# Row factors through DRAM in place of diagonal products and a second turn of k, in a hybrid encoder layer on one core

## The chip, the core and the metric

The kernel runs on one core of a Trainium2 chip. The metric is the device time of one launch in microseconds; a smaller number is better. The engines are named PE (TensorE), DVE (VectorE), ACT (ScalarE), POOL (GpSimd) and SP (SyncE, which here issues DMAs alone). Each engine takes its instructions in the order in which the program has them, and waits where one of them waits.

## The reference

One layer, 512 tokens of 2048 channels, all in float32.

```python
h = rms_norm(x, norm_g[layer])
proj = jnp.einsum('bsd,de->bse', h, w_in[layer])
qa, ka, va, ga, qb, kb, vb, gb = jnp.split(proj, splits, axis=-1)
ya = stick_breaking_attention(...)      # branch A, 8 heads of 128
yb = chunk_band_attention(...)          # branch B, 8 heads of 128
mixed = jnp.concatenate([merge_heads(ya) * jax.nn.silu(ga),
                         merge_heads(yb) * jax.nn.silu(gb)], axis=-1)
x = x + jnp.einsum('bse,ed->bsd', mixed, w_out[layer])
```

Two factors of this matter here. `rms_norm(x)` divides each token by the root of its mean square: one number a token, here called `rstd`. In branch B, `chunk_band_attention` begins with `q = rms_norm(q, q_gain)` and `k = rms_norm(k, k_gain)`, over the 128 channels of a head: again one number a token, for each head.

## The kernel before, in words

The two large products, with `w_in` and with `w_out`, make up nearly all of PE's work. Each number is split into a high and a low part, and a product is made of three of the four products of parts; blocks are combined by a Winograd scheme with seven products in place of eight. The product with `w_in` is cut into 32 units (8 groups of two heads; in each group q, k, v and gate), and most units are 7 stages of 16 matmuls (L866 and L868 in the profile). For each stage, weights are loaded from DRAM by SP (L520, L536), some are summed by a DMA that POOL issues (L540, L559) or by DVE (L548), then ACT makes the high part (L579) and DVE the low part (L580), which is called a split here. DVE and ACT also bring the products out of the banks of PSUM and combine them (L612 to L649).

Odd groups belong to branch B, even ones to branch A. The attention of a head runs beside the large product of later units, on three spare banks. A head's number is n = 2g + h for group g and h = 0 or 1.

The projections come out with channels on the 128 partitions and 512 tokens along the row (`C`). A factor by token is then a number by column, and no engine's operand by partition can hold it. The kernel before deals with that in two ways:

- `R` is `rstd` as a row, the same in all partitions: [128, 512]. `x_rstd` makes four diagonal blocks out of `rstd` (L1277), PE multiplies a block of ones with them (L1284, in `spread`), and DVE copies the bank into `R`. All that takes R into account waits for it.
- For q and k of branch B, `prep_b` turns the head on PE, so that tokens lie on the partitions (four transposes of 128 x 128, L1429, reading `c`); ACT squares the turned head and sums along the row (L1434), and small operations of 4 columns make the factor `y` (L1442, L1443, `rsqrt` with L1226 to L1233, L1447). For k, ACT then scales the turned head by `y` into a buffer `tm` (L1461), and PE turns it back (L1429 again, reading `tm`). `heads` splits the result into high and low part (L1470, L1471).

For q the factor goes into the softmax and needs no row.

The order of all engines is made when the program is built. A planner (`schedule`) plays the work through with a cost for each operation and a clock of its own; on each engine it takes the ready operation that is due first. An `Op` on SP counts as done when its bytes and a landing time have gone by. `landing(us)` holds a piece of work back for some more time of that clock. What comes out is a fixed order on each engine; on the chip the instructions wait by semaphores. Weight loads are asked for about 10 us before their stage. `buffer(tag)` hands out room in the tags L (one buffer), W (three) and bias (one); `take` and `give` hand out the three spare banks.

`done.add(("read", n, kind))` marks that q (0) or k (1) of a head has been read out of `C`, whose tile the next group may then overwrite, and the next head's `prep_b` waits for it.

Of the kernel before, what the change touches and what calls it, by code (L numbers as in the profile page):

```python
# [8 lines left out]
F32 = mybir.dt.float32  # L9
# [68 lines left out]
def trunk_kernel(ctx: ExitStack, tc: tile.TileContext, xT, xn, wi, wqk, wo, ng, qg, kg, rel, out):  # L78
# [51 lines left out]
    halves = banks.rearrange("p a (b c) -> p (a b) c", c=H)  # L130
    mixd = [dp.tile([P, S], F32, tag=f"mixd{i}", name=f"mixd{i}") for i in range(2 * NG)]
# [1114 lines left out]
    def x_stat(t, i, k):  # L1246
        x = []

        def fn():
            x.append(tmp([P, S], "W", "xs", bufs=3))  # L1250
# [6 lines left out]
        drop("W", k)  # L1257
        done.add(("stat", t, i))

    def x_rstd():  # L1260
# [11 lines left out]
        ks = yield from buffer("W", 2)  # L1272
        o = tmp([P, P], "W", "ones", bufs=3)
        d = tmp([P, S], "W", "diag", bufs=3)
        yield G(0.3, lambda: pool.memset(o, 1.0))
        for t in range(NT):
            yield DV(128, lambda: dve.tensor_scalar(out=d[:, t * P:(t + 1) * P], in0=ident, scalar1=rstd[:, t:t + 1], scalar2=None,  # L1277
                                                   op0=ALU.mult), 0.0)
        i = yield from take("R")

        def spread():
            for t in range(NT):
                s_ = slice(t * P, (t + 1) * P)
                pe.matmul(banks[:, i, s_], o, d[:, s_], start=True, stop=True)  # L1284

        yield M(1.0, spread)
        for k in ks:
            drop("W", k)
        yield DV(512, lambda: dve.tensor_copy(R, banks[:, i, :]), 0.0)
        give(i)  # L1290
        done.add("R")
# [123 lines left out]
    def prep_b(g, kind, h):  # L1415
# [316 lines left out]
```

## Time and profile before

| | us |
|---|---|
| median of 3 runs | 901.56 (901.37 to 901.56) |
| profiled execution | 901.53 |
| its span, first to last instruction | 899.6 |

| engine | busy us | share of the span |
|---|---|---|
| PE | 892.7 | 99% |
| DVE | 767.7 | 85% |
| ACT | 658.8 | 73% |
| POOL | 69.9 | 8% |

The granted clock of PE is 1.00 throughout. The sixteen DMA engines move 177 GB/s on average. In a row of the profile, `L866 PE MATMUL banks<-x,parts ... xN | busy, mean | idle <-who` gives the source line, engine, operation, what is written and read, the count, the busy time in us and the mean duration of one in ns, then the idle time of the engine just before these and what ended it. A row of the timeline begins with the start in us and the length in us. Matmuls overlap: the next starts before the one ahead has ended. Of DMAs, the last number is the median time from issue to landing, in us.

### The profile page before, as it was taken

Reading aid. Unit: us, or ns where it says so; the run is one execution under the profiler, and the core shown is the slowest. Engines: PE = TensorE matmul, PEld = TensorE weight load, DVE = VectorE, ACT = ScalarE, POOL = GpSimd, SP = SyncE. Lnnn points to the kernel's source line nnn. Section 1 sums busy time; section 2 is a strip of 40 time slices with the busy share of each in tenths; the row PEclk is TensorE's granted clock in tenths of the full one; section 3 lists DMA queues with packets and bytes.
Section 4 is the critical chain, followed back from the end, with each engine's and each line's share of the span. In section 5 each row is a group of like instructions: output and inputs, shape, how many; then the busy total and the mean of one; then the engine's idle time right before and its main releaser. Section 6 shows DMA issues by size and latency. Waiting matters only on the chain.

```text
span 899.6 us, 15403 instructions
## 1 busy us (share of the span) xinstructions
PE 892.7 (99%) x5456; PEld 796.5 (89%) x5456; DVE 767.7 (85%) x1257; ACT 658.8 (73%) x1225; POOL 69.9 (8%) x96
## 2 busy tenths in 40 slices
PE   9999999999999999999999999999999999999998
PEld 7898888888888888888888888888888988999997
DVE  7998989787887977988889778888888988988785
ACT  7876968797698858986978588869878885544342
POOL 0001000000000000000000100000000000101012
PEclk9999999999999999999999999999999999999999
DMA  9777786868679888776878777868775536656371
GB/s 312 250 212 164 159 178 178 194 148 202 161 171 173 196 190 162 192 186 161 184 168 201 191 172 182 191 158 185 167 165 136 178 118 208 158 195 180 126 188 47
DMA packets 200509, 159.36 MB, mean 177 GB/s; under 512 B 21744, under 2 KB 170224, under 8 KB 200432
## 3 DMA queue, kind: packets, MB, share of 16 engines
q1 hardware_dynamic: 190352, 125.73, 48.1%
q0 software_dynamic: 9792, 32.51, 22.4%
q8 instruction: 43, 0.70, 0.3%
q14 instruction: 34, 0.28, 0.1%
q10 hardware_dynamic: 288, 0.14, 0.1%
HBM read 117.45 MB, written 8.39 MB: 140 GB/s over the span
## 4 chain that ended last, share of the span: by engine, by line
PE 95%; ACT 2%; DMA 1%; issue 1%; DVE 1%; SPq 0%; DVEq 0%; ACTq 0%
PE banks L866 39%; PE banks L795 21%; PE banks L868 19%; PE banks L793 10%; PE banks L1523 2%; PE banks L856 2%; PE banks L1429 1%; PE banks L857 1%; DMA arena<-in_wi 1%; ACT parts L579 0%; ACT W L1499 0%; DMA xq<-in_xT 0%; ACT W L1506 0%; PE banks L1355 0%; PE banks L1570 0%
## 5 line engine op out<-in xcount | busy, mean ns | idle before, releaser
L866 PE MATMUL banks<-x,parts 128*128 128x512 f32 x1568 | 501.1, 401 | 0.2 <-DVE arena L622 0.2
L868 PEld LDWEIGHTS banks<-x,parts 128*128 128x128 f32 x1568 | 294.3, 188 | 70.5 <-DVE parts L580 1.0
L868 PE MATMUL banks<-x,parts 128*128 128x256 f32 x1568 | 309.8, 279 | 0.3 <-DVE parts L580 0.3
L580 DVE TENSOR_TENSOR parts<-arena,parts 128x1024 fp32r<-128x1024 f32 x196 | 238.8, 1220 | 52.7 <-ACT parts L579 51.8
L579 ACT CAST parts<-arena 128x1024 fp32r<-128x1024 f32 x196 | 205.7, 1050 | 86.3 <-PE banks L866 46.2
L866 PEld LDWEIGHTS banks<-x,parts 128*128 128x128 f32 x1568 | 240.4, 189 | 1.3 <-issue 0.4
L795 PE MATMUL banks<-parts,x 128*128 128x256 f32 (+1 forms) x672 | 134.5, 298 | 0.0
L458 ACT CAST parts<-arena 128x1024 fp32r<-128x1024 f32 (+2 forms) x86 | 77.1, 908 | 69.2 <-PE banks L795 38.2
L795 PEld LDWEIGHTS banks<-parts,x 128*128 128x128 f32 x672 | 107.5, 191 | 3.7
L462 DVE TENSOR_TENSOR parts<-arena,parts 128x1024 fp32r<-128x1024 f32 (+2 forms) x86 | 89.0, 1044 | 14.5 <-ACT parts L458 14.5
L793 PE MATMUL banks<-parts,x 128*128 128x256 f32 (+1 forms) x336 | 100.3, 299 | 0.0
L548 DVE TENSOR_TENSOR arena<-arena 128x1024 f32<-128x1024 f32 x56 | 68.2, 1218 | 16.0 <-DMA arena<-in_wi 15.5
L795 PE MATMUL banks<-x,parts 128*128 128x256 f32 (+1 forms) x320 | 74.9, 326 | 0.1
L793 PEld LDWEIGHTS banks<-parts,x 128*128 128x128 f32 x336 | 63.9, 190 | 3.2
L795 PEld LDWEIGHTS banks<-x,parts 128*128 128x128 f32 x320 | 54.0, 190 | 5.6 <-DVE parts L462 0.7
L793 PE MATMUL banks<-x,parts 128*128 128x256 f32 (+1 forms) x160 | 52.9, 330 | 0.0
L540 POOL DMA_DIRECT2D arena<-arena x28 | 24.4, 873 | 327.9 <-DVE arena L622 71.8
L622 DVE TENSOR_TENSOR arena<-banks,arena 128x512 f32<-128x512 f32 x56 | 38.1, 681 | 5.3 <-PE banks L868 5.1
L559 POOL DMA_DIRECT2D arena<-arena x28 | 24.3, 868 | 232.2 <-DVE parts L580 178.3
L1532 DVE TENSOR_TENSOR wtl<-banks,wth 128x128 fp32r<-128x128 f32 (+1 forms) x64 | 31.0, 484 | 3.0 <-ACT wth L1531 2.8
L793 PEld LDWEIGHTS banks<-x,parts 128*128 128x128 f32 x160 | 30.5, 190 | 3.1 <-ACT parts L458 0.3
L1523 PE MATMUL banks<-ident,W 128*128 128x128 f32 x160 | 28.1, 274 | 0.8 <-ACT W L1508 0.7
(216 smaller groups left out, 1181.0 us busy)
## 6 DMA issues: line engine op xcount, KB each, us to landing
arena<-in_wi SPq DMA_DIRECT2D x308, 256.0 KB, 4.6
arena<-arena POOLq DMA_DIRECT2D x56, 512.0 KB, 5.7
arena<-in_wo SPq DMA_DIRECT2D x64, 256.0 KB, 3.1
xs<-in_xn SPq DMA_DIRECT2D x16, 256.0 KB, 4.2
mixd<-c SPq DMA_DIRECT2D x16, 256.0 KB, 3.5
out<-co SPq DMA_DIRECT2D x16, 256.0 KB, 4.6
x<-mixd SPq DMA_DIRECT2D x12, 256.0 KB, 4.0
co<-in_xn POOLq DMA_DIRECT2D x12, 256.0 KB, 6.0
```

The source lines that it names most:

```text
L458: act.copy(whl[n, part][:, 0, c], t)
L462: yield DV(c.stop - c.start, lambda: dve.tensor_tensor(out=l[:, c], in0=t, in1=h[:, c].bitcast(F32), op=ALU.subtract), need(k, 0.5))
L548: add = lambda x, due: DV(1024, lambda: dve.tensor_tensor(out=r("A21"), in0=r("A21"), in1=r(x), op=ALU.add), due)
L579: yield AC(1024, lambda: act.copy(v[:, 0, :], t), need(k, AHEAD[3]))
L580: yield DV(1024, lambda: dve.tensor_tensor(out=v[:, 1, :], in0=t, in1=v[:, 0, :].bitcast(F32), op=ALU.subtract), need(k, AHEAD[4]))
L622: join = lambda i, x, y, op=ALU.subtract: lambda: dve.tensor_tensor(out=c[:, i, :], in0=x, in1=y, op=op)
L793: pe.matmul(o, lh, rh, start=start, stop=False, **kw)
L795: pe.matmul(o, x, y, start=False, stop=stop and (x is ll) != early, **kw)
L866: pe.matmul(both, mats[n][:, 0, j, :], X[j][:, :, i, :], start=p in (0, 1, 5) and j == 0, stop=False, skip_group_check=True)
L868: pe.matmul(o[:, :H], mats[n][:, 1, j, :], X[j][:, 0, i, :], start=False, stop=j == NJ - 1, skip_group_check=True)
L1523: pe.transpose(t[:, j * P:(j + 1) * P], src[:, j * P:(j + 1) * P], ident)
L1532: yield DV(w, lambda: dve.tensor_tensor(out=tl[:, blocks, :], in0=tv, in1=th[:, blocks, :].bitcast(F32), op=ALU.subtract))
```

## The change

`as_row` is new. It writes the factor, a tile of 128 partitions and 4 columns, to a row of 512 numbers in DRAM (`rowd`, one for each head and one for `rstd`), waits, and reads that row back into all 128 partitions with a step of 0 between partitions. Both transfers are issued by SP.

- `R` comes from `as_row`; ones, diagonal blocks, their product and the copy are gone.
- k of branch B in groups 1, 3 and 5 is turned once, for its squares. The squares are written back into the bank, which is given back at once. The factor becomes a row (`kr`), DVE multiplies the unturned head in `C` by it in place, and `heads` reads `C` instead of the bank. Group 7 (`NG - 1`) keeps the two turns.
- q's squares go into the bank too, and need no buffer L.
- What the next `prep_b` waits for is a new mark, `squares`; `read` for k comes after `heads`.
- The 16 loads of x for `rstd` use buffers of the tags L and bias beside W: five in flight in place of three.

```diff
     def x_stats():
         yield lambda: position[0] > 18
         for t in range(NT):
             for i in range(4):
-                k, = yield from buffer("W")
-                spawn(x_stat(t, i, k), (0, 1))
+                tag = ("W", "W", "L", "W", "bias")[(4 * t + i) % 5]
+                k, = yield from buffer(tag)
+                spawn(x_stat(t, i, tag, k), (0, 1))
...
     def x_rstd():
...
-        ks = yield from buffer("W", 2)
-        o = tmp([P, P], "W", "ones", bufs=3)
-        d = tmp([P, S], "W", "diag", bufs=3)
-        yield G(0.3, lambda: pool.memset(o, 1.0))
-        for t in range(NT):
-            yield DV(128, lambda: dve.tensor_scalar(out=d[:, t * P:(t + 1) * P], in0=ident, scalar1=rstd[:, t:t + 1], scalar2=None,
-                                                   op0=ALU.mult), 0.0)
-        i = yield from take("R")
-
-        def spread():
-            for t in range(NT):
-                s_ = slice(t * P, (t + 1) * P)
-                pe.matmul(banks[:, i, s_], o, d[:, s_], start=True, stop=True)
-
-        yield M(1.0, spread)
...
-        yield DV(512, lambda: dve.tensor_copy(R, banks[:, i, :]), 0.0)
-        give(i)
+        yield from as_row(rstd, R, rowd[2 * NG])
         done.add("R")
+
+    def as_row(columns, row, at):
+
+        w = NT * P * 4
+        yield L_(w, lambda: sp.dma_start(at.rearrange("(t p) -> p t", p=P), columns, allow_slow_non_contiguous=True))
+        yield landing(0.3)
+        yield L_(P * 2048, lambda: sp.dma_start(row, bass.AP(tensor=at.tensor, offset=at.offset, ap=[[0, P], [1, S]])))
...
     def prep_b(g, kind, h):
...
-        yield lambda: all(("read", n - 1, k) in done for k in range(2)) if h else kind == 0 or ("read", n, 0) in done
-        yield lambda: not h or kind == 0 or ("read", n, 0) in done
-        k, = yield from buffer("L")
-        t_ = tmp([P, S], "L", "tm")
+        yield lambda: all(("squares", n - 1, k) in done for k in range(2)) if h else kind == 0 or ("squares", n, 0) in done
+        yield lambda: not h or kind == 0 or ("squares", n, 0) in done
         i = yield from take(("forth", g, kind, h))
...
+        by_rows = kind == 0 or g < NG - 1
+        o = b
+        if not by_rows:
+            k, = yield from buffer("L")
+            o = r = tmp([P, S], "L", "kr")
         for t in range(NT):
-            yield Op("ACT", 0.5, lambda: act.activation(t_[:, t * P:(t + 1) * P], b[:, t * P:(t + 1) * P], AF.Square,
+            yield Op("ACT", 0.5, lambda: act.activation(o[:, t * P:(t + 1) * P], b[:, t * P:(t + 1) * P], AF.Square,
                                                         accum_out=ssq[:, kind, h, t:t + 1]))
+        if by_rows:
+            give(i)
...
-        for t in range(NT):
-            yield Op("ACT", 0.37, lambda: act.activation(t_[:, t * P:(t + 1) * P], b[:, t * P:(t + 1) * P], AF.Copy, scale=y[:, t:t + 1]))
-        d = yield from qk_of(g, h)
-        yield M(0.5, lambda: turn_(t_))
-        drop("L", k)
-        yield from heads(n, 1, d, b, kg_t)
-        give(i)
...
+        k, = yield from buffer("L")
+        r = tmp([P, S], "L", "kr")
+        yield from as_row(y, r, rowd[n])
+        yield DV(512, lambda: dve.tensor_tensor(out=f, in0=f, in1=r, op=ALU.mult))
+        drop("L", k)
+        d = yield from qk_of(g, h)
+        yield from heads(n, 1, d, f, kg_t)
+        done.add(("read", n, 1))
```

Since the planner plays the whole program through again, the order changes on every engine, while the large products keep theirs. Three places are shown. In the changed file the lines of the stages are one higher (L866 becomes L867, L580 becomes L581), and the numbers behind `x_` differ by name alone.

On PE, the place in group 3 where the second turn of k of its first head stood. Before:

```order
L868 MATMUL banks<-x_143,parts 128x256
L868 MATMUL banks<-x_145,parts 128x256
L1429 MATMUL banks<-ident,tm 128x128 x4
L866 MATMUL banks<-x_204,parts 128x512
L866 MATMUL banks<-x_206,parts 128x512
```

Now, at the same place of the large product:

```order
L869 MATMUL banks<-x_160,parts 128x256
L869 MATMUL banks<-x_162,parts 128x256
L867 MATMUL banks<-x_221,parts 128x512
L867 MATMUL banks<-x_223,parts 128x512
L869 MATMUL banks<-x_221,parts 128x256
```

The four transposes are gone and nothing has come in their place.

On SP, where group 3's two heads have their rows made (`rowd` is the row in DRAM, `rq` the factor, `kr` the row in all partitions; the other rows are loads of weights, a store of a finished head and a DMA transpose of v). Now:

```order
L537 DMA arena<-in_wi 128x4x128 x2
L521 DMA arena<-in_wi 128x4x128 x6
L1280 DMA rowd_88<-rq 128x4x1
L521 DMA arena<-in_wi 128x4x128 x2
L1282 DMA kr<-rowd_88 128x512
L537 DMA arena<-in_wi 128x4x128 x2
L1544 DMA_TRANSPOSE vt<-c_3384 128x8x128
L521 DMA arena<-in_wi 128x4x128 x4
L1280 DMA rowd_89<-rq 128x4x1
L521 DMA arena<-in_wi 128x4x128 x2
L1282 DMA kr<-rowd_89 128x512
L521 DMA arena<-in_wi 128x4x128 x2
```

Before, the same stretch of loads was

```order
L536 DMA arena<-in_wi 128x4x128 x2
L520 DMA arena<-in_wi 128x4x128 x8
L536 DMA arena<-in_wi 128x4x128 x2
L1539 DMA_TRANSPOSE vt<-c_3362 128x8x128
L520 DMA arena<-in_wi 128x4x128 x8
```

Each write and its read stand among the weight loads, with two loads between them here, and everything behind the read is issued after it.

On DVE, the first head of group 3 again, from the last product of k's factor (L1443, before L1447) to the product with the row (L1467), in two pieces. Now:

```order
L1443 TENSOR_TENSOR rq<-rq,rstd 128x4
L623 TENSOR_TENSOR arena<-arena,banks 128x512
L581 TENSOR_TENSOR parts<-arena,parts 128x1024
L1438 TENSOR_TENSOR vq<-ssq,rstd_75 128x4
L1439 TENSOR_SCALAR vq<-vq 128x4
L623 TENSOR_TENSOR arena<-banks,arena 128x512
L581 TENSOR_TENSOR parts<-arena,parts 128x1024
L1231 TENSOR_TENSOR nwt<-rq 128x4
L1232 TENSOR_TENSOR nwt<-nwt,vq 128x4
L1233 TENSOR_SCALAR nwt<-nwt 128x4
L1234 TENSOR_TENSOR rq<-rq,nwt 128x4
```

and, next to it,

```order
L549 TENSOR_TENSOR arena<-arena 128x1024
L1443 TENSOR_TENSOR rq<-rq,rstd 128x4
L1447 TENSOR_SCALAR yn<-rq 128x4
L1448 RECIPROCAL yi<-rq 128x4
L1438 TENSOR_TENSOR vq<-ssq,rstd_75 128x4
L1439 TENSOR_SCALAR vq<-vq 128x4
L642 TENSOR_TENSOR arena<-arena 128x2x256
L1467 TENSOR_TENSOR c_3186<-c_3186,kr 128x512
L581 TENSOR_TENSOR parts<-arena,parts 128x1024
L642 TENSOR_TENSOR arena<-arena 128x2x256
L581 TENSOR_TENSOR parts<-arena,parts 128x1024
L1476 SCALAR_TENSOR_TENSOR qk_2994<-c_3186,kg_t,qk_2994 128x512
```

Before, the same head had no such product:

```order
L1447 TENSOR_TENSOR rq<-rq,rstd 128x4
L622 TENSOR_TENSOR arena<-banks,arena 128x512
L580 TENSOR_TENSOR parts<-arena,parts 128x1024
L548 TENSOR_TENSOR arena<-arena 128x1024
L641 TENSOR_TENSOR arena<-arena 128x2x256
L580 TENSOR_TENSOR parts<-arena,parts 128x1024
L641 TENSOR_TENSOR arena<-arena 128x2x256
L580 TENSOR_TENSOR parts<-arena,parts 128x1024
L1471 SCALAR_TENSOR_TENSOR qk_3000<-banks,kg_t,qk_3000 128x512
```

The product with the row stands right ahead of a split (L581). In group 5 the rows are the same; in group 1 the stretch has five operations of 1024 columns, four of 512 and nine of 4; in the second heads of each group it has four splits and more.

More of the change, by code (lines that the diff above doesn't have):

```diff
@@ L130, in trunk_kernel @@
     halves = banks.rearrange("p a (b c) -> p (a b) c", c=H)
+    rowd = [dp.tile([S], F32, tag=f"rowd{i}", name=f"rowd{i}") for i in range(2 * NG + 1)]
     mixd = [dp.tile([P, S], F32, tag=f"mixd{i}", name=f"mixd{i}") for i in range(2 * NG)]
@@ L1241, in x_stats, with x_stat @@
             for i in range(4):
-                k, = yield from buffer("W")
-                spawn(x_stat(t, i, k), (0, 1))
+                tag = ("W", "W", "L", "W", "bias")[(4 * t + i) % 5]
+                k, = yield from buffer(tag)
+                spawn(x_stat(t, i, tag, k), (0, 1))
                 yield lambda: ("stat", t, i, "load") in done
-    def x_stat(t, i, k):
+    def x_stat(t, i, tag, k):
         x = []
         def fn():
-            x.append(tmp([P, S], "W", "xs", bufs=3))
+            x.append(tmp([P, S], tag, "xs", bufs=3 if tag == "W" else 1))
             sp.dma_start(x[0], xn[t][:, i * S:(i + 1) * S])
@@ L1256, in x_stat @@
         yield AC(512, lambda: act.activation(x_, x_, AF.Square, accum_out=ssx[:, t * 4 + i:t * 4 + i + 1]), 75.0)
-        drop("W", k)
+        drop(tag, k)
         done.add(("stat", t, i))
@@ L1431, in prep_b @@
         yield M(0.5, lambda: turn_(f))
+        by_rows = kind == 0 or g < NG - 1
[3 more added lines that the diff above has]
+            o = r = tmp([P, S], "L", "kr")
         for t in range(NT):
-            yield Op("ACT", 0.5, lambda: act.activation(t_[:, t * P:(t + 1) * P], b[:, t * P:(t + 1) * P], AF.Square,
+            yield Op("ACT", 0.5, lambda: act.activation(o[:, t * P:(t + 1) * P], b[:, t * P:(t + 1) * P], AF.Square,
                                                         accum_out=ssq[:, kind, h, t:t + 1]))
+        if by_rows:
+            give(i)
         if kind == 0:
-            give(i)
-        done.add(("read", n, kind))
+            done.add(("read", n, kind))
+        done.add(("squares", n, kind))
         v, y = vq[:, kind, h, :], rq[:, kind, h, :]
@@ L1458, in prep_b @@
             return
-        for t in range(NT):
-            yield Op("ACT", 0.37, lambda: act.activation(t_[:, t * P:(t + 1) * P], b[:, t * P:(t + 1) * P], AF.Copy, scale=y[:, t:t + 1]))
+        if not by_rows:
+            for t in range(NT):
+                yield Op("ACT", 0.37, lambda: act.activation(r[:, t * P:(t + 1) * P], b[:, t * P:(t + 1) * P], AF.Copy, scale=y[:, t:t + 1]))
+            d = yield from qk_of(g, h)
+            yield M(0.5, lambda: turn_(r))
+            drop("L", k)
+            yield from heads(n, 1, d, b, kg_t)
+            done.add(("read", n, 1))
+            give(i)
+            return
+        k, = yield from buffer("L")
+        r = tmp([P, S], "L", "kr")
+        yield from as_row(y, r, rowd[n])
+        yield DV(512, lambda: dve.tensor_tensor(out=f, in0=f, in1=r, op=ALU.mult))
+        drop("L", k)
         d = yield from qk_of(g, h)
-        yield M(0.5, lambda: turn_(t_))
-        drop("L", k)
-        yield from heads(n, 1, d, b, kg_t)
-        give(i)
+        yield from heads(n, 1, d, f, kg_t)
+        done.add(("read", n, 1))
     def heads(n, kind, d, x, scale):
```

2 lines of the change are left out of this document (removed).

## The prediction

> **What bounds the kernel now.** I read the page first: engine shares, the chain of waits, the groups.
>
> ```profile
> span 899.6 us, 15403 instructions
> PE 892.7 (99%) x5456; PEld 796.5 (89%) x5456; DVE 767.7 (85%) x1257; ACT 658.8 (73%) x1225; POOL 69.9 (8%) x96
> PE 95%; ACT 2%; DMA 1%; issue 1%; DVE 1%; SPq 0%; DVEq 0%; ACTq 0%
> L866 PE MATMUL banks<-x,parts 128*128 128x512 f32 x1568 | 501.1, 401 | 0.2 <-DVE arena L622 0.2
> L868 PE MATMUL banks<-x,parts 128*128 128x256 f32 x1568 | 309.8, 279 | 0.3 <-DVE parts L580 0.3
> ```
>
> TensorE (PE) is busy for 99% of the span, the chain runs through it for 95%, and its two costliest groups stood idle for 0.2 and 0.3 us in all. So the order on PE sets the time, and every matmul taken out of it is worth the time until the next one can start. The other engines count only where they make PE wait. The profiled execution took 901.53 us, 1.93 us more than its span, and agrees with the median of the three runs, 901.56 us; I sum against 901.53.
>
> **What leaves PE.** The next question is what one turn costs, and a duration does not tell it, because matmuls overlap. These are the groups by source line, then the timeline of PE around the second turn of one k:
>
> ```profile
> L1429 PE MATMUL banks<-ident,c x64: 270/273/274, 121.6 to 689.9; 128*128 128x128 f32 x64
> L1429 PE MATMUL banks<-ident,tm x32: 271/273/294, 167.5 to 715.5; 128*128 128x128 f32 x32
> ...
> 166.57 0.40 PE L868 MATMUL banks<-x,parts 128*128 128x256 f32 x2
> ...
> 166.80 0.63 PE L866 MATMUL banks<-x,parts 128*128 128x512 f32 x2
> ...
> 167.27 0.41 PE L868 MATMUL banks<-x,parts 128*128 128x256 f32 x2
> ...
> 167.51 0.60 PE L1429 MATMUL banks<-ident,tm 128*128 128x128 f32 x4
> ...
> 167.87 0.71 PE L866 MATMUL banks<-x,parts 128*128 128x512 f32 x2
> ...
> 168.41 0.40 PE L868 MATMUL banks<-x,parts 128*128 128x256 f32 x2
> ```
>
> Without a turn, the pairs on L868 start 0.70 us apart (166.57, 167.27). With it they start 1.14 us apart (167.27, 168.41). So four transposes cost 0.44 us, not the 4 x 0.273 = 1.1 us of their durations. The 32 on `tm` are eight turns, one for each head of branch B; the edit keeps two, those of the last group, so six go: 6 x 0.44 = 2.64 us. The first turns, the 64 on `c`, all stay, because the squares are still taken from them.
>
> The diagonal product is priced in the same way:
>
> ```profile
> 69.33 0.40 PE L795 MATMUL banks<-x,parts 128*128 128x256 f32 x2
> ...
> 69.57 1.06 PE L1284 MATMUL banks<-diag,ones 128*128 128x128 f32 x8
> ...
> 70.38 0.70 PE L866 MATMUL banks<-x,parts 128*128 128x512 f32 x2
> ...
> 70.93 0.40 PE L868 MATMUL banks<-x,parts 128*128 128x256 f32 x2
> ```
>
> A pair on L866 takes 0.47 us to the next L868 (166.80 to 167.27 above). Counted back from 70.93 the pair could have started at 70.46, where without the product it starts at 69.57: 0.89 us. PE loses 2.64 + 0.89 = 3.53 us of work.
>
> **What leaves and joins the others.** ScalarE (ACT) loses the six scaled copies out of the bank, VectorE (DVE) the four diagonal blocks and a copy of R, and gains six products with the row:
>
> ```profile
> L1461 ACT ACTIVATE tm<-banks,rq 128x128 f32<-128x128 f32 x32 | 10.1, 366 | 0.0
> L1277 DVE TENSOR_SCALAR diag<-ident,rstd 128x128 f32<-128x128 f32 x4 | 1.6, 463 | 0.0
> L1342 DVE TENSOR_TENSOR c<-c,R 128x512 f32<-128x512 f32 x8 | 5.2, 683 | 0.0
> ```
>
> ACT: 24 x 0.366 = 8.8 us less. DVE: 6 x 0.68 = 4.1 us more, 1.6 + 0.7 us less. Both lie beside PE, with ACT 73% and DVE 85% busy, so I put them at nothing. The remaining edits, the squares written back into the bank and five buffers for the statistics, change when things start and not how much is done; the latter sends two more loads of 256 KB ahead of weights between 22 and 30 us, in the second of these 40 slices:
>
> ```profile
> GB/s 312 250 212 164 159 178 178 194 148 202 161 171 173 196 190 162 192 186 161 184 168 201 191 172 182 191 158 185 167 165 136 178 118 208 158 195 180 126 188 47
> ```
>
> I take 0 for them, between 0 and about 2 us (512 KB at 250 GB/s) if those weights had no spare time.
>
> **What is new: two transfers in a row, and two engines that wait in order.** Seven times SP (the DMA queue) now issues a write of 512 single numbers to DRAM, two to four other loads, and then a read that must wait for the write's landing. Behind that read stand weight loads; behind the product with the row, on DVE, stand the splits (L580 before) that feed PE. No row shows a write of single numbers. The nearest are a load of 128 single numbers, stores of whole rows, and the bias load, which reads the same size into 128 partitions:
>
> ```profile
> mixd<-c SPq DMA_DIRECT2D x16, 256.0 KB, 3.5
> bias<-in_rel SPq DMA_DIRECT2D x8, 256.0 KB, 5.2
> kg_t<-in_kg SPq DMA_DIRECT2D x1, 0.5 KB, 3.8
> L1656 SPq DMA_DIRECT2D kg_t<-in_kg x1: 422/422/422, 24.0 to 24.0; - x1
> ```
>
> I take 3.8 + 5.2 = 9.0 us from the issue of the write to the landing of the row. What does DVE have to do in that time? The prices, by group:
>
> ```profile
> L580 DVE TENSOR_TENSOR parts<-arena,parts 128x1024 fp32r<-128x1024 f32 x196 | 238.8, 1220 | 52.7 <-ACT parts L579 51.8
> L548 DVE TENSOR_TENSOR arena<-arena 128x1024 f32<-128x1024 f32 x56 | 68.2, 1218 | 16.0 <-DMA arena<-in_wi 15.5
> L622 DVE TENSOR_TENSOR arena<-banks,arena 128x512 f32<-128x512 f32 x56 | 38.1, 681 | 5.3 <-PE banks L868 5.1
> L641 DVE TENSOR_TENSOR arena<-arena 128x512 f32<-128x512 f32 x12 | 8.2, 685 | 0.1
> L1231 DVE TENSOR_TENSOR nwt<-nwt,vq 128x4 f32<-128x4 f32 x16 | 2.6, 163 | 0.6
> ```
>
> In the changed order the shortest stretch on DVE between the last product of the factors and the product with the row is that of the first heads of groups 3 and 5: two L622, two L580, one L548, one L641 and eleven operations of 4 columns, 1.4 + 2.4 + 1.2 + 0.7 + 1.8 = 7.5 us. That of group 1 is five of 1.22, four of 0.68 and nine small ones, 10.3 us; the second heads and R have 12 us and more. So the row comes late twice, by 9.0 - 7.5 = 1.5 us, less where DVE waits for other things on its way.
>
> What does such a wait cost PE? The trace has one that can be followed from SP to PE: a DMA transpose holds SP, the load behind it is late, DVE waits, PE starts late.
>
> ```profile
> L1539 SPq DMA_TRANSPOSE vt<-c x12: 1260/1596/3294, 169.6 to 640.6; - x12
> ...
> 282.74 3.25 SPq L1539 DMA_TRANSPOSE vt<-c  x1
> ...
> 286.04 10.92 SPq L520 DMA_DIRECT2D arena<-in_wi  x6
> ...
> 292.71 1.23 DVE L548 TENSOR_TENSOR arena<-arena 128x1024 f32<-128x1024 f32 x1 [3.08 <-DMA arena<-in_wi]
> ...
> 294.04 0.39 PE L868 MATMUL banks<-x,parts 128*128 128x256 f32 x2
> 294.68 0.70 PE L866 MATMUL banks<-x,parts 128*128 128x512 f32 x2 [0.25 <-DVE arena L622]
> 295.72 0.51 PE L868 MATMUL banks<-x,parts 128*128 128x256 f32 x2 [0.34 <-DVE parts L580]
> ```
>
> At the pace above, the pair of 295.72 follows that of 294.04 after 0.70 us, at 294.74. PE lost 0.98 us, where DVE waited 3.08: the splits stand far enough ahead that 2.1 us of a wait cost nothing. The two late rows, at 1.5 us, then cost 0, which is also the lower bound, since a row that comes early gains nothing; the upper one is in the first rival.
>
> The hold on SP costs more. The read is issued 3.8 us after the write; two loads stand between them at 0.42 us each, so SP stands still for about 3.0 us, seven times, as long as the longest transpose did. Of the twelve transposes one passed 0.98 us on, or 0.08 us each, and by that rate seven holds cost 0.6 us; the bounds are 0 and 7 x 0.98 = 6.9 us. I take 0.5 us, near the rate, because the weights behind are asked for some 10 us ahead (the planner's due times).
>
> [...]
>
> **The sum.** 901.53 - 2.64 - 0.89 + 0.5 = 898.5 us, 0.34% less.
>
> **The rivals.**
>
> Slower: the write of single numbers is the slow part. 512 pieces of 4 bytes are four times those of `kg_t`, and they go to DRAM. If it lands after 7.6 us, twice that row, the row is there after 12.8 us: late by 5.3 us in two heads and by 2.5 us in one, which costs 2 x (5.3 - 2.1) + 0.4 = 6.8 us, and the time is 901.53 - 3.53 + 6.8 = 904.8. It decides from 7.1 us of landing on: then two waits of 4.8 us cost PE the 5.3 us that lie between the work saved and 0.2% slower. For it: nothing of this kind was measured. Against it: in the order shown ahead each weight load (`128x4x128`) has 512 pieces as well, of 512 bytes, and stores of 256 KB to DRAM land in 3.5 us. [...] I give 0.11.
>
> No change: the loads behind the read have less to spare than the transposes' neighbours. If half of the seven holds pass on what the one at 282.74 did, 3.4 us go, and the time is 901.4. For it: the idle time on the row of L548 is 15.5 us of waiting for weights, so some loads already come just in time, and the two early loads of the statistics push the same way. 0.19.
>
> Faster still: the new order also drops waits that PE has now. One is the 0.98 us above, the other this one, where the transposes of weights wait for ACT:
>
> ```profile
> 223.67 0.40 PE L868 MATMUL banks<-x,parts 128*128 128x256 f32 x2
> 224.51 0.55 PE L1523 MATMUL banks<-ident,W 128*128 128x128 f32 x3 [0.45 <-ACT W L1508]
> ```
>
> The next start after a pair on L868 is due 0.23 us later (166.57 to 166.80), at 223.90; it came 0.61 us late. ACT has 8.8 us less to do in branch B's groups, and this wait is in one of them. Without either wait and without new ones: 901.53 - 3.53 - 0.98 - 0.61 = 896.4 us. Against it: any new order brings waits of its own. 0.13.
>
> **How the numbers follow.** The forecast, 898.5, has 0.57; its own range is 898.0 (no new wait) to 899.7. About 0.2% or 1.8 us is what a measurement of this kernel can tell from no change, so faster means below 899.76 and slower above 903.36. Faster is 0.57 + 0.13 = 0.70, the same 0.19, slower 0.11. For 8 in 10 the range goes from 896.4, where the third rival lies, up to 902.3: that takes in most of the second rival, which spreads from 899.8 to 903.3, and leaves out the first.
>
> **What would show it.** PE work: the diagonal product is gone, the turn of k on the same line as the first turns remains with 8 matmuls on `kr` and 64 on `c`, and PE's busy time falls by about 3.5 us to 889. Waits: DVE idles before the product with the row at most 1.5 us, in the first heads of groups 3 and 5; the write of the row lands in about 3.8 us and the read in about 5.2. SP: each read waits about 3 us for its write, and DVE's idle time for weights, 15.5 us on the row of L548, grows by a few microseconds, while PE shows no more than 1 us of new idle time. The forecast is wrong if PE's busy time does not fall, which would mean that the turns were not in its way; or if PE's idle time rises by over 2 us, with DVE behind the row's read or behind weights as the releaser; then the place names which rival it is.

## The result, and the profile after

The changed kernel takes 939.09 us (936.91 to 941.39 in four runs) beside 901.56 us before: 1.0416 times the time, interval 1.039 to 1.0443. The forecast was 898.5 us with a range of 896.4 to 902.3. It was wrong in sign: 37.5 us slower.

On the page of the changed kernel (its lines are one higher than before: L867 and L869 are the matmuls that were L866 and L868, L581 the split that was L580) stand the span, PE's share, the chain of waits by engine and the two costliest groups:

```profile
span 939.5 us, 15350 instructions
PE 904.4 (96%) x5424; PEld 802.9 (85%) x5424; DVE 770.3 (82%) x1258; ACT 658.9 (70%) x1203; POOL 69.6 (7%) x95
PE 73%; DMA 13%; DVE 6%; ACT 4%; issue 3%; SPq 1%; DVEq 0%; ACTq 0%
L867 PE MATMUL banks<-x,parts 128*128 128x512 f32 x1568 | 507.3, 405 | 8.1 <-ACT arena L617 4.9
L869 PE MATMUL banks<-x,parts 128*128 128x256 f32 x1568 | 313.6, 282 | 12.5 <-DVE parts L581 12.5
```

PE has 32 matmuls less, but is busy for 11.7 us more and idle for 35.1 us of the span, where it was idle for 6.9. The chain runs through DMAs for 13%, where it did for 1%. The list of DMA issues (median from issue to landing) and the waits say which:

```profile
arena<-in_wi SPq DMA_DIRECT2D x308, 256.0 KB, 4.9
kr<-rowd SPq DMA_DIRECT2D x6, 256.0 KB, 6.3
rowd<-rq SPq DMA_DIRECT2D x6, 2.0 KB, 9.6
```

```profile
DVE c L1467 <- DMA kr<-rowd: 24.9, 6, 7.2
PE banks L869 <- DVE parts L581: 12.5, 4, 5.0
```

The write of 2 KB lands after 9.6 us and the read after 6.3, DVE waits for the row in all six heads, up to 7.2 us at a time, and PE waits behind it. One of the six, the first head of group 3, in the timeline of SP, DVE and PE:

```profile
350.71 0.38 SPq L1280 DMA_DIRECT2D rowd<-rq  x1
352.45 1.98 SPq L521 DMA_DIRECT2D arena<-in_wi  x2
359.66 0.33 SPq L1282 DMA_DIRECT2D kr<-rowd  x1
...
363.88 0.69 DVE L1467 TENSOR_TENSOR c<-c,kr 128x512 f32<-128x512 f32 x1 [6.15 <-DMA kr<-rowd]
364.49 1.22 DVE L581 TENSOR_TENSOR parts<-arena,parts 128x1024 fp32r<-128x1024 f32 x1
...
361.02 0.40 PE L869 MATMUL banks<-x,parts 128*128 128x256 f32 x2
...
365.76 0.80 PE L869 MATMUL banks<-x,parts 128*128 128x256 f32 x2 [3.88 <-DVE parts L581]
367.21 0.63 PE L869 MATMUL banks<-x,parts 128*128 128x256 f32 x2
368.49 0.56 PE L869 MATMUL banks<-x,parts 128*128 128x256 f32 x2
369.35 0.40 PE L869 MATMUL banks<-x,parts 128*128 128x256 f32 x2
```

SP stands from 354.43 to 359.66, the row is there 13.2 us after the write's issue, and PE stops for 3.88 us. Then the pairs on L869 come 1.45, 1.28 and 0.86 us apart, not 0.70: PE pays another 1.5 us after the stop. Stretches of the same trace show both causes (per row: the stretch, its length, busy time of PE, PEld, DVE, ACT, POOL, PE's granted clock, DMA share, GB/s):

```profile
351.00:353.00 2.00, 2.00 (x13) 1.73 (x13) 1.97 (x5) 0.95 (x3) 0.86 (x1) 1.00 1.06 239
...
355.00:357.00 2.00, 2.00 (x14) 1.74 (x13) 1.88 (x8) 1.37 (x4) 0.00 (x0) 1.00 1.18 37
357.00:359.00 2.00, 2.00 (x14) 1.73 (x13) 0.73 (x2) 1.85 (x3) 0.00 (x0) 1.00 0.61 59
359.00:361.00 2.00, 2.00 (x13) 1.76 (x12) 0.00 (x0) 1.35 (x3) 0.00 (x0) 1.00 0.45 46
361.00:363.00 2.00, 0.89 (x5) 0.42 (x3) 0.00 (x0) 0.00 (x0) 0.00 (x0) 1.00 0.91 252
...
365.70:369.10 3.40, 3.34 (x11) 2.94 (x12) 2.50 (x4) 2.75 (x4) 0.86 (x1) 0.54 0.50 96
369.10:373.00 3.90, 3.90 (x24) 3.42 (x23) 3.43 (x9) 2.67 (x6) 0.00 (x0) 1.00 1.33 211
```

For the six microseconds from 355 to 361 all sixteen DMA engines together move 37 to 59 GB/s, though two weight loads of 256 KB were issued from 352.45 on. And after the stop PE is granted about half its clock for 3.4 us. The mean clock of the whole execution is 0.987, and 939.5 x 0.013 = 12 us is the most that this can have cost; six times the 1.5 us of this stop are 9. So 9 to 12 us of the loss are the half clock, as an estimate.

The two spans differ by 39.9 us. Set against the same main matmuls before, PE is 2.2 us late from the ninth us on, ahead of any row; the other versions of the changed order are within 0.5 us there, and this execution is the slowest of the four. It is 7.1 us late at 110 us of the kernel before, 14.0 at 320, 26.5 at 500, 38.0 at 610 and 39.6 at 760. That is 4.9 us more behind R's row and 6.9, 12.5 and 11.5 behind the rows of groups 1, 3 and 5: 35.8 of the 39.9 us sit where the seven rows are.

### The profile page after: what moved, and what is told of

Read it like the earlier page. It is cut to its first block, busy times and chain, and to the rows that moved or that the text cites. A ratio compares the mean times of both kernels' runs of the same rounds, so it can differ in the third digit from the quotient of the medians.

```text
span 939.5 us, 15350 instructions
## 1 busy us (share of the span) xinstructions
PE 904.4 (96%) x5424; PEld 802.9 (85%) x5424; DVE 770.3 (82%) x1258; ACT 658.9 (70%) x1203; POOL 69.6 (7%) x95
## 4 chain that ended last, share of the span: by engine, by line
PE 73%; DMA 13%; DVE 6%; ACT 4%; issue 3%; SPq 1%; DVEq 0%; ACTq 0%
PE banks L867 30%; PE banks L796 16%; PE banks L869 15%; PE banks L794 8%; DMA rowd<-rq 4%; DMA arena<-in_wi 3%; DMA kr<-rowd 2%; DVE parts L581 2%; PE banks L1528 2%; PE banks L857 1%; DMA arena<-arena 1%; DMA rowd<-rstd 1%; ACT parts L580 1%; DMA R<-rowd 1%; DVE parts L463 1%
## 5 line engine op out<-in xcount | busy, mean ns | idle before, releaser
L867 PE MATMUL banks<-x,parts 128*128 128x512 f32 x1568 | 507.3, 405 | 8.1 <-ACT arena L617 4.9
L869 PEld LDWEIGHTS banks<-x,parts 128*128 128x128 f32 x1568 | 298.5, 191 | 85.4 <-DVE parts L581 14.6
L869 PE MATMUL banks<-x,parts 128*128 128x256 f32 x1568 | 313.6, 282 | 12.5 <-DVE parts L581 12.5
L580 ACT CAST parts<-arena 128x1024 fp32r<-128x1024 f32 x196 | 205.4, 1050 | 100.2 <-PE banks L867 65.7
L581 DVE TENSOR_TENSOR parts<-arena,parts 128x1024 fp32r<-128x1024 f32 x196 | 238.4, 1220 | 43.1 <-ACT parts L580 41.6
L867 PEld LDWEIGHTS banks<-x,parts 128*128 128x128 f32 x1568 | 244.4, 192 | 10.3 <-ACT arena L617 5.3
L796 PE MATMUL banks<-x,parts 128*128 128x256 f32 (+1 forms) x320 | 76.1, 330 | 0.2 <-DVE parts L463 0.2
L796 PEld LDWEIGHTS banks<-x,parts 128*128 128x128 f32 x320 | 54.8, 193 | 6.0 <-DVE parts L463 0.7
L794 PE MATMUL banks<-x,parts 128*128 128x256 f32 (+1 forms) x160 | 53.7, 336 | 0.1
L794 PEld LDWEIGHTS banks<-x,parts 128*128 128x128 f32 x160 | 30.8, 193 | 3.9 <-ACT parts L459 0.8
```

What stands on the lines that cost most here:

```text
L580: yield AC(1024, lambda: act.copy(v[:, 0, :], t), need(k, AHEAD[3]))
L581: yield DV(1024, lambda: dve.tensor_tensor(out=v[:, 1, :], in0=t, in1=v[:, 0, :].bitcast(F32), op=ALU.subtract), need(k, AHEAD[4]))
L794: pe.matmul(o, lh, rh, start=start, stop=False, **kw)
L796: pe.matmul(o, x, y, start=False, stop=stop and (x is ll) != early, **kw)
L867: pe.matmul(both, mats[n][:, 0, j, :], X[j][:, :, i, :], start=p in (0, 1, 5) and j == 0, stop=False, skip_group_check=True)
L869: pe.matmul(o[:, :H], mats[n][:, 1, j, :], X[j][:, 0, i, :], start=False, stop=j == NJ - 1, skip_group_check=True)
```

## The experiments

The theory after the traces had three parts: (1) the write is slow, because its pieces of 4 bytes lie side by side; (2) while it lasts, other transfers stand too; (3) late rows and late weights stop PE, six times for 3.2 to 5.4 us between two starts, and half the clock follows each of the six. Against it: the write is slow by its number of pieces, or by the load around it; SP's hold alone does the harm; the new order of the work does.

### The write by itself

The kernel before, with one write of `rstd` ahead of seven of the eight bias loads, each in another form; nothing waits for them.

```diff
+        def fn():
+            if n in probe:
+                sp.dma_start(*probed(n), allow_slow_non_contiguous=True)
+            sp.dma_start(b, bass.AP(tensor=row.tensor, ...))
```

> The kernel before, with seven writes of rstd to rooms of their own in DRAM, each issued by SP right ahead of a bias load; nothing waits for what they write. Forms: 512 pieces of 4 bytes next to each other as in the change (twice), 512 pieces 64 bytes apart, 512 pieces 512 bytes apart, 128 pieces of 16 bytes, 256 pieces of 8 bytes, 128 pieces of 4 bytes. In the changed kernel the write landed after 8.9 to 12.1 us. Theory 1a (pieces that fall into the same lines of DRAM are written one after the other): the two adjacent forms land after 9 to 10 us, those that are spread after 4 to 5. Theory 1b (each piece has a price, wherever it goes; (9.6 - 3.5) us / 512 = 12 ns): the spread forms land after 9 to 10 us too, 256 pieces after 6.5, 128 pieces of either size after 5. Theory 2 (the landing is long because of the load on the queue around it, and not because of its pieces): all seven land alike, with the same spread as neighbouring loads, 4 to 6 us. The time grows by what the stop of the DMA engines costs, up to 5 us.

It took 903.7 us in its one run, beside 901.99. The landings, one of each form and two of the first:

| form | us from issue to landing |
|---|---|
| 512 pieces of 4 bytes side by side, twice | 10.6 and 9.9 |
| 128 pieces of 4 bytes side by side | 10.7 |
| 256 pieces of 8 bytes side by side | 6.1 |
| 128 pieces of 16 bytes side by side | 5.1 |
| 512 pieces of 4 bytes, 64 bytes apart | 3.8 |
| 512 pieces of 4 bytes, 512 bytes apart | 5.0 |

A quarter of the pieces lands as late, and all 512 of them, 64 bytes apart, land as early as the load of `kg_t` did before. So neither the number of pieces nor their size sets the time, but how close together they lie. In 64 bytes, the smallest distance tried at which the write was fast, lie 1, 4, 8 or 16 of the pieces, and these forms took 3.8, 5.1, 6.1 and 10.6 us: some 0.3 to 0.45 us for each piece more. Distances between 4 and 64 bytes were not tried. (The step from 64 to 512 bytes apart, 3.8 to 5.0 us, has no explanation here; it is about as large as the one from 1 piece to 4.) The stretches behind the first form, issued at 136.16, and behind the one 64 bytes apart, issued at 192.51:

```profile
138.00:140.00 2.00, 2.00 (x12) 1.70 (x11) 2.00 (x4) 2.00 (x6) 0.00 (x0) 1.00 0.81 182
140.00:142.00 2.00, 2.00 (x14) 1.73 (x13) 2.00 (x3) 2.00 (x4) 0.00 (x0) 1.00 0.90 11
142.00:144.00 2.00, 2.00 (x14) 1.73 (x13) 2.00 (x4) 1.35 (x2) 0.67 (x1) 1.00 1.09 14
144.00:146.00 2.00, 2.00 (x15) 1.82 (x14) 2.00 (x4) 1.92 (x3) 0.21 (x1) 1.00 0.65 16
...
194.50:196.50 2.00, 2.00 (x13) 1.73 (x13) 1.09 (x1) 2.00 (x5) 0.00 (x0) 1.00 0.94 185
196.50:198.50 2.00, 2.00 (x15) 1.78 (x14) 1.84 (x8) 1.97 (x4) 0.15 (x1) 1.00 0.72 206
```

Side by side, the DMA engines move 11 to 16 GB/s for six microseconds; 64 bytes apart, 185 to 206. The bias load behind the slow forms lands after 8.4 to 9.0 us, behind the others after 4.2 to 5.7.

### Sixteen bytes in a piece

In the changed kernel the four numbers of a partition go to DRAM as one piece; the row comes out in another order, and DVE's product puts it right. For R one more copy on DVE does that.

```diff
-        yield L_(w, lambda: sp.dma_start(at.rearrange("(t p) -> p t", p=P), columns, allow_slow_non_contiguous=True))
+        yield L_(w, lambda: sp.dma_start(at.rearrange("(p t) -> p t", p=P), columns, allow_slow_non_contiguous=True))
...
-        yield DV(512, lambda: dve.tensor_tensor(out=f, in0=f, in1=r, op=ALU.mult))
+        yield DV(512, lambda: dve.tensor_tensor(out=f.rearrange("q (t p) -> q t p", p=P), in0=f.rearrange("q (t p) -> q t p", p=P), in1=r.rearrange("q (p t) -> q t p", p=P), op=ALU.mult))
```

> The change with one size changed: the factor goes to DRAM as it lies in SBUF, 128 pieces of 16 bytes, and the row is read back as before; its order is put right by a step of four in the product with the row (for R by one more copy on DVE of 0.7 us). Theory 1 (the 512 single pieces make the loss): the write lands after about 5 us instead of 9.6, DVE's waiting for the row falls from 24.9 us to under 8, and the time to 898 to 905 us. Theory 2 (two transfers in a row through DRAM, with the wait on SP between them, are too long whatever their pieces): still over 925 us.

906.33 us, 1.0038 times the kernel before (1.0021 to 1.0054). DMA issues, and the wait for the row:

```profile
kr<-rowd SPq DMA_DIRECT2D x6, 256.0 KB, 4.5
...
rowd<-rq SPq DMA_DIRECT2D x6, 2.0 KB, 4.4
```

```profile
DVE c L1471 <- DMA kr<-rowd: 3.2, 3, 1.4
```

Bytes and queue are the same, SP still waits for each write before it issues the read, and 32.8 of the 37.5 us are gone; the time is 1.3 us above theory 1's range. The extra copy for R makes the planner choose another order up to about 250 us. Behind that the order of every engine is the same as in the changed kernel: from 320 us of the kernel before to the end the changed kernel falls another 25.8 us behind the kernel before (39.8 - 14.0), this one 5.1. The pieces side by side are shown as the cause of nearly all of the loss; SP's hold as such is not. The permuted row has a price of its own: the product with it takes 1.10 us in the median, where it took 0.69.

### No write at all

The writes are left out and the row is read from an input, so the factors are wrong; the order of every engine is that of the changed kernel.

```diff
-        yield L_(w, lambda: sp.dma_start(at.rearrange("(t p) -> p t", p=P), columns, ...))
+        yield L_(w, lambda: None)
-        ... bass.AP(tensor=at.tensor, offset=at.offset, ...)
+        ... bass.AP(tensor=xn.tensor, offset=xn.offset, ...)
```

> The change without the seven writes; the row is read from an input instead, at the same place in the order, so the factors are wrong, and SP never waits ahead of the read. PE's work is that of the change. Theory 1 (write): 897 to 901 us, DVE waits for the row at most 2 us at a time. Theory 2 (the read as such, at 6.3 us, is late as well): over 910 us. Theory 3 (the new order costs it, with or without late rows): over 925 us.

903.22 us in one run. That is 35.9 us less than with the writes, in the same order, so the writes are what costs; but it is above theory 1's 901. Without any write and any hold of SP, the changed order is 1.2 us above before, not 3.5 us below. Against the same main matmuls before it is 1.5 us ahead at 320 us, level at 500 and 610, and 1.6 us late at 760, behind group 7, where the changed kernel loses 1.6 as well. DVE's waits for the row, and the longest of PE's:

```profile
DVE c L1467 <- DMA kr<-in_xn: 5.2, 3, 2.2
PE banks L1528 <- ACT W L1513: 3.2, 5, 1.4
```

So the work that left PE did not come out as time. That became the second question.

### A planner that knows

The change with 7.0 us for the landing in place of 0.3: the planner sets the read, and the product with the row, later.

```diff
-        yield landing(0.3)
+        yield landing(7.0)
```

> The change with 7.0 in place of 0.3 in the planner's wait between write and read, so that SP issues other loads ahead of the read and DVE's product with the row stands later in the order. If the loss comes from the place of the read and of the product in the order (theory 3, a plan that knows the true landing cures it): 897 to 905 us. If the write itself stops the DMA engines for some 7 us, seven times (theory 1), weights stay late: SP's wait for the write shrinks from 34 us to under 10, but the time stays above 910 us.

921.7 us in one run: 17 of 37.5 us come back. DVE's wait for the row falls to 3.9 us in two heads and SP's wait for the write from 34.4 to 19.3 us (not under 10), but the write still lands after 9.4 us. Knowing the delay makes the row less late; the loss that remains fits theory 1.

### Another queue

The change, with write and read on GpSimd's queue; SP is never held. The planner's waits are changed too (3.1 us behind the write, 3.3 behind the read), so the order is another one.

```diff
-        yield L_(w, lambda: sp.dma_start(at.rearrange(...
+        yield G(1.2, lambda: pool.dma_start(at.rearrange(...
-        yield L_(P * 2048, lambda: sp.dma_start(row, ...
+        yield G(1.2, lambda: pool.dma_start(row, ...
```

> The change with the writes of single numbers and the reads of the rows issued by GpSimd on its own queue instead of by SP; the pieces stay at 4 bytes, side by side, and the planner counts 4.4 us for the write. SP is never held for a row. Theory a (the slow write stops the DMA engines for every queue): the weight loads that SP issues within some 3 us behind a write still land only after 9 to 11 us, PE keeps its stops of 3 us and more at weights, 925 to 940 us. Theory b (only the queue with the write stands still, and SP's hold did the rest): the write still lands after 9 to 10 us and the products with the row wait 4 to 6 us, but weights land in 4 to 6 us, and the time falls to 908 to 920 us.

959.8 us in one run, the slowest of all and beyond what either theory said. The weight loads that SP issued between 190 and 197 us, around a write by GpSimd at 189.73 (first to last start; then minimum, median and maximum to landing), and the stretches behind it:

```profile
L521 SPq DMA_DIRECT2D arena<-in_wi x6: 540/593/650, 189.5 to 196.2; - x6
...
DMA to landing us min/median/max: 3.8/11.7/13.6
```

```profile
191.00:193.00 2.00, 2.00 (x13) 1.82 (x12) 1.85 (x6) 2.00 (x7) 0.00 (x0) 1.00 1.13 222
193.00:195.00 2.00, 2.00 (x14) 1.78 (x13) 1.88 (x5) 1.90 (x5) 0.00 (x0) 1.00 0.33 98
195.00:197.00 2.00, 2.00 (x13) 1.74 (x13) 0.66 (x2) 2.00 (x5) 0.00 (x0) 1.00 0.27 10
197.00:199.00 2.00, 2.00 (x12) 1.66 (x10) 0.00 (x0) 1.92 (x4) 0.00 (x0) 1.00 0.65 14
```

Only the load issued ahead of the write landed as usual, after 3.8 us. The others, on a queue that had nothing to do with the write, took up to 13.6. So theory a holds where the two differ: the loads of a queue without the write stand too, and all sixteen DMA engines together moved 10 and 14 GB/s from 195 to 199 us. What makes this version slower still is probably GpSimd's own hold, which has the sums of weights behind it; that was not tried by itself. The waits have it as

```profile
POOL kr L1282 <- DMA rowd<-rq: 38.3, 4, 11.3
```

### The work taken from PE, and nothing else

The kernel before in its order, with the six second turns and the diagonal product left out (so R and six heads' factors are wrong).

```diff
-        yield M(0.5, lambda: turn_(t_))
+        yield M(0.5, (lambda: turn_(t_)) if g == NG - 1 else lambda: None)
-                pe.matmul(banks[:, i, s_], o, d[:, s_], start=True, stop=True)
+                pass
```

> The kernel before in its own order, with the six second turns of k and the diagonal product simply left out; R is copied from the diagonal blocks and k's heads read the first turn, so the factors of R and of six heads are wrong. This measures the work that leaves PE by itself. Theory (PE sets the pace, a turn is worth 0.44 us and the diagonal product 0.89 us): 3.5 us less than before, 898.5 us beside 902.0, PE busy about 889. Rival (VectorE or ScalarE takes over as soon as PE has less to do, so that the work taken from PE was worth nothing): 901.5 to 902.

901.4 us in ten runs (899.24 to 903.51), 0.9997 times the kernel before (0.9987 to 1.0006). The work is gone and the time has stayed, close to the rival's number. In the timeline of PE the product's place is closed up as forecast:

```profile
69.83 0.63 PE L866 MATMUL banks<-x,parts 128*128 128x512 f32 x2
70.30 0.39 PE L868 MATMUL banks<-x,parts 128*128 128x256 f32 x2
```

From 69.83 to L868 are 0.47 us, where 69.57 to 70.93 were 1.36: 0.89 us less, the size forecast. Against the same matmuls before, PE also gains 0.45 us at each turn. But by 76.5 us 0.6 of the first gain are lost again, at 248 us 1.7, and at 295 us 0.4. The first place, in the timelines of DVE and PE of this run, and then of the kernel before:

```profile
75.20 1.22 DVE L580 TENSOR_TENSOR parts<-arena,parts 128x1024 fp32r<-128x1024 f32 x1
76.47 0.51 PE L868 MATMUL banks<-x,parts 128*128 128x256 f32 x2
...
75.20 1.22 DVE L580 TENSOR_TENSOR parts<-arena,parts 128x1024 fp32r<-128x1024 f32 x1
76.50 0.47 PE L868 MATMUL banks<-x,parts 128*128 128x256 f32 x2
```

DVE works here without a break from 71 to past 80 us, at the same times in both kernels, to 0.01 us, from 72.5 us on. Its split ends at 76.42, and a PE that is ahead cannot start its matmuls sooner. No weight is waited for. The second place is another: the chain of waits of this run between 243 and 250 us, in order of time.

```profile
238.50 6.81 DMA arena<-in_wi
...
245.40 0.10 DVE arena L548
...
247.22 1.13 DVE parts L580
248.35 0.27 DVE W L1403
...
249.01 0.33 PE banks L1523
```

It begins with a weight load of 6.81 us: DVE waits for it, ACT's softmax step waits for DVE behind it, and PE's transposes wait for ACT. The same load was issued 0.52 us later before, at 239.02, and landed after 5.1 us; DVE waited 0.9 us for it there and 2.7 here. So the load was not asked for too late; it took longer, and whether a PE that is ahead brings that about or chance is open. At 295 us the transpose by DMA that holds SP, in the prediction's own example, comes before the late load again. Over the kernel DVE's wait for weights on L548 rises from 15.5 to 20.2 us in as many places. A PE that is ahead meets engines and transfers that are not.

### Weights that come sooner

Before, and the run without the work, both with the twelve transposes by DMA replaced by plain transfers of the same bytes, which hold SP for 0.7 us in the median instead of 1.6 (v is not turned).

```diff
-        sp.dma_start(turned.rearrange("p (a b) -> p a b", b=P), planes, transpose=True)
+        sp.dma_start(turned, planes)
```

> The kernel before, in its own order, with the twelve transposes by DMA replaced by plain transfers of the same bytes (v is not turned, so the output is not the reference's). SP is then held for about 0.5 us instead of 1.3 to 3.3 us each time. Alone it shows what those holds cost: if only the wait at 295 us comes from them, about 1 us, so 900.5 to 901; if they set the pace of branch B, more.

> Both at once: the work taken from PE (six turns of k, the diagonal product) and plain transfers in the place of the transposes, order as before. Theory (the work taken from PE came to nothing because SP, held by transposes, asked for weights too late for a faster PE): now the work counts, 897 to 898.5 us, which is 2.5 to 3.5 us below the plain transfers alone. Rival (ScalarE's and VectorE's chain in branch B's heads takes the time back, whatever SP does): within 1 us of the plain transfers alone.

900.66 us (0.9984, 0.9975 to 0.9993) with the work, as expected, and 899.54 us (898.02 to 901.12; 0.9976, 0.9964 to 0.9987) without it. The work is now worth 1.1 us in the medians and 0.95 in the means, with a 95% interval of about 0 to 1.9 us; in the profiled execution, the fastest of its kind at 898.02, 2.0 of the six turns' 2.6 us stay to the end, and the diagonal product's gain is lost again by 76 us. The theory's 2.5 to 3.5 us did not come out, and 1.1 is hardly more than the rival's 1 us. That the transposes which hold SP are part of why the work was worth nothing is suggested by this, and not shown: the gain without them, 1.1 beside 0.3 us, lies within the spread of 3 us of these runs.

### A better 16-byte version

The 16-byte form, with a planner that counts 1.2 us more for the write and 1.0 more for the read (`landing(1.5)`, and `landing(1.0)` ahead of the product).

> The 16-byte form with a planner that counts 1.2 us more for the write and 1.0 us more for the read, so that it places the product with the row where the row is there. Theory (of the 8 us between this form's 906.3 and the 898.5 of the forecast, the late row is the part of about 3 us, and the rest is other waits of the new order): waits of VectorE for the row fall from 3.2 us to under 1 us, and 902 to 904 us. Rival (the late row is nothing, the order of the ScalarE chain in branch B is all): the row's waits go, and the time stays at 905.5 to 907. A version faster than before (under 900.5) would need the new order to bring no waits at all.

903.87 us, 1.0021 (1.0005 to 1.0037). No product waits for a row of k among the longest waits, and the theory's number is met; it is still not faster than before.

### R alone

The kernel before, with R alone made by a row of 16-byte pieces.

```diff
+        yield L_(w, lambda: sp.dma_start(rowd.rearrange("(p t) -> p t", p=P), rstd, ...))
+        yield landing(1.5)
+        yield L_(P * 2048, lambda: sp.dma_start(r, bass.AP(tensor=rowd.tensor, ..., ap=[[0, P], [1, S]])))
+        yield DV(512, lambda: dve.tensor_copy(R.rearrange("q (t p) -> q t p", p=P), r.rearrange("q (p t) -> q t p", p=P)), 0.0)
```

> The kernel before with only R made by a row: one write in 128 pieces of 16 bytes, one read, one VectorE copy that puts the columns in order; k keeps its two turns and the statistics their three buffers. Theory (work leaves PE and one hold of SP of about 4 us on 16-byte pieces costs next to nothing, since the order is hardly touched): 0.9 us less than before, 900.9 to 901.6. Rival (any transfer pair in this place upsets more than it saves): 902.3 or more, with an idle stretch of PE over 1 us between 60 and 100 us.

909.48 us, 1.009 (1.0075 to 1.0105). That is within the rival's number, but not at its place: between 75 and 150 us the main matmuls came some 1.2 us earlier than before (the median; other work of PE has moved, so single ones came 0.3 to 3.6 us earlier), and R's row cost nothing there. From 165 us on they came late, 7.5 us in the end. PE's timeline there:

```profile
165.93 0.27 PE L796 MATMUL banks<-wth,v 128*128 128x128 f32 x1
168.30 0.66 PE L1419 MATMUL banks<-ident,tm 128*128 128x128 f32 x4 [2.10 <-ACT tm L1451]
170.02 1.22 PE L867 MATMUL banks<-x,parts 128*128 128x512 f32 x2 [1.06 <-ACT arena L613]
```

The new order puts the second turn of group 1's first k half as many products behind its first turn as before; the scaled copies were not ready, and PE's granted clock was 0.61 in the mean from 168.3 to 172 us and 0.51 from 172 to 176. A planner that counts 0.8 us after the write (`landing(0.8)`) makes another order there:

> R alone by a row of 16-byte pieces again, with a planner that counts 0.8 us instead of 1.5 us after the write. That puts the second turn of the first k of group 1 about three times as many products behind its first turn as in the run before, where PE stood idle there. Theory (the row of R itself costs nothing; its 3.0 us of lead at 156 us were lost by the order at that one place): no idle stretch of PE over 2 us between 150 and 190 us, and 899 to 901.5 us. Rival (the row of R itself costs the time, for example by the buffers or SP): 904 or more, with the loss between 60 and 100 us.

900.27 us in eleven runs, 0.9983 (0.9974 to 0.9991): 0.17% less than before, with an interval that just excludes 1. It is the one version here that computes the layer and takes less time than both kernels, and one of two orders tried. No wait of PE is left between 150 and 190 us, as the theory said. R's row and the 0.89 us of work that leaves PE are the same in both runs; the 9.2 us between them come with the order.

## Why the prediction was wrong

**What bounds the kernel.** "Every matmul taken out of it is worth the time until the next one can start" fails. PE busy for 99% of the span does not mean that PE alone sets the pace. Without the work the kernel took the same time (0.9997), because other limits lie close behind PE, another one at each place: DVE at work without a break at 76 us, a weight load that landed 1.7 us slower at 248, a hold of SP at 295, with DVE waiting 3.5 us for the load behind it. The prediction put DVE "at nothing" because it is 85% busy; that is an average, and from 72.5 to 80 us it is 100%.

**What leaves PE, 3.53 us.** Both sizes were right where they stand, 0.89 us for the product and 0.45 for a turn. Their worth was wrong: 0.3 us by themselves, by the interval between 1.2 us less and 0.5 us more, and 1.1 us with faster transfers on SP. Even a free write would not have brought 898.5: without one the change took 903.2.

**The step that failed for the sign is the first of the two in "3.8 + 5.2 = 9.0 us".** The write took 9.6 us in the kernel, and the read 6.3 instead of 5.2. The row for the write was chosen by the number of pieces (`kg_t`, 128 of them), and the 128 of `kg_t` were read from DRAM; no row had numbers written side by side there. With 16-byte pieces the write landed after 4.4 us and the read after 4.5, 8.9 us in all: for that form this term would have been right.

**Two late rows at 1.5 us, free up to 2.1 us.** Late were all six, by up to 7.2 us. The rate "2.1 us are free and the rest counts once" gives 4.05 us for the head shown, where DVE waited 6.15, and PE stood still for 3.88. What it leaves out comes behind the stop: 1.5 us at half the clock there, some 9 to 12 us in all, which no term of the sum had.

**SP's hold, 0.5 us.** Seven holds were counted at 3.0 us each; SP waited 34.4 us for five of the six writes of k's factors. But not the hold was mis-sized most: what goes on behind it was not in the sum at all, the loads in flight that stand still with the write (37 to 59 GB/s in all for six microseconds), those of another queue too (up to 13.6 us to landing). The 16-byte form keeps the hold, shorter (9.1 us for four of the six), and loses little.

**Off the path: ACT and DVE.** ACT's group of scaled copies fell from 10.1 to 2.9 us as counted, but its busy time stayed, 658.9 us for 658.8; why is open. Of the changed order, left without its writes, 1.2 us more than before remain although PE has less to do; the waits on ACT's softmax step suggest its chain, and that is argued, not shown.

**The rivals.** The slower one, at 0.11, had the right place, the write, and its condition was met: a landing beyond 7.1 us. At the measured 9.6 us its rule gives 7.3 us of lateness twice, 4.5 once and some 2.8 four times, less 2.1 each: 2 x 5.2 + 2.4 + 4 x 0.7 = 15.6 us, 913.6 us. The other 25 us are not in its rule: the halted weights, the half clock and the order. This rival took the number of the pieces for the cause, four times those of `kg_t`; but 512 pieces of 4 bytes landed after 3.8 us when they lay 64 bytes apart, and 128 of them side by side after 10.7. What counts in these runs is that they lie close together. The faster rival said against itself that "any new order brings waits of its own"; the two runs of R alone, 909.5 and 900.3 us, show how large that can be.

**What would show it.** The prediction named PE's idle time with DVE behind the row's read as the sign of this rival, and that is what the page shows: L869, 12.5 us behind L581. PE's busy time did not fall to 889 but rose to 904.4, above all because half the clock lengthens matmuls: from 365.7 to 369.1 us, at 0.54, those of 128x512 took 580 ns in the mean, and 400 in the 3.9 us behind it, at 1.00; without the halts, in the 16-byte form with the better planner, it was 891.6.

## What to carry to other kernels

Before small numbers go to DRAM, count how many pieces lie next to each other, and join them in the writer: 16 pieces in 64 bytes took 10 us here, with loads of another queue landing after up to 13.6 us, and the permuted row costs the reader only 0.4 us for each product. PE at 99% hid a second bound here (3.5 us of its work left out, 0.9997 times the time), so look stage by stage at the work and the waits of the engines that feed it, and leave the work out once, in an unchanged order, before a saving on it is counted. Where a planner makes the order, a change of 0.7 us in one of its numbers moved this kernel by 9 us; a version is judged with its order, not by the work that it saves.

## What the runs showed of the hardware

- Writes to DRAM in pieces that share 64 bytes take some 0.3 to 0.45 us longer for each piece more, an estimate from one or two landings of each form: 3.8 us for one piece, 10.6 for sixteen. For about six of these microseconds the sixteen DMA engines moved 10 to 60 GB/s, where the mean of the changed kernel is 172, and loads of another queue landed after up to 13.6 us. Where in the machine this happens, and whether 64 bytes is the exact bound, stays open.
- In the changed kernel, after each of six stops of PE with 3.2 to 5.4 us between two starts (at 82, 177, 204, 366, 558 and 588 us) the granted clock was 0.5 for some 3.4 us, once (at 558) for 6.8; after the stops of 2.5 and 2.2 us at 388 and 395 us it stayed at 1.00. The other runs show no sharp line between the two: with 7.0 us in the planner a stop of 3.1 us between two starts, at 190.7 us, left the clock at 1.00; and in the slower run of R alone a stop of 2.4 us, four transposes and another 1.1 us of idle PE were followed by 0.51 between 172 and 176 us.
